# Hybrid attention and mixture-of-experts layer: the gate's low-rank columns join another product, and the blocks of the last norm take other turns

## The chip, the cores and the metric

The kernel runs on one core of one Trainium2 chip. The metric is the device time of one execution in microseconds (us); lower is better. A core has five engines that work from queues of their own and wait for one another through semaphores: TensorE (PE, matrix products; loads of its stationary operand are listed as PEld), VectorE (DVE), ScalarE (ACT), GpSimd (POOL) and SyncE (SP). SBUF is the core's working memory, PSUM the small memory that products write to, HBM the main memory. All transfers share 16 DMA engines.

## The reference

One decoder layer over 2048 tokens of 1024 numbers, in float32, and a last norm. Cut to what the change touches:

```python
n = rmsnorm(h, norm1_g)
proj = n @ w_in                       # (2048 x 1024) @ (1024 x 3088)
gq, gk, gv, gr, glr, aq, ak, av = jnp.split(proj, IN_SPLITS, axis=-1)   # gr: 512 columns, glr: 16
log_a = jax.nn.log_sigmoid(glr @ gla_gate_w2 + gla_gate_b) / GLA_TAU    # low-rank forget gate
...                                   # linear attention, its output times silu(gr); dilated window attention
h = h + o @ w_out
h = h + hier_moe(rmsnorm(h, norm2_g), ...)
return rmsnorm(h, final_norm_g)

def hier_moe(n, ...):                 # 4 groups of 8 experts: one group a token, two experts in it
    ...
    hb = silu(xb @ w1[e]) * (xb @ w3[e])     # 1024 -> 512
    return hb @ w2[e]                        # 512 -> 1024, times the gate, summed into the token
```

A token's group is the best of four, and both its experts are of that group. So a token of group 0 or 1 is finished after expert 15, one of group 2 after expert 23, one of group 3 after its later expert.

## The kernel before, in words

**Products in float32.** An operand is split into a rounded part (hi) and the rest (lo), and each product is made of three: hi with hi, hi with lo, lo with hi.

**The front (`front`).** The tokens are normed in 16 tiles of 128 (`norm_tile`) and transposed into quarters of 512 tokens, `nh` and `nl`. Columns of `w_in` come in groups of 256 (`w_group`): load into `raw`, split on ScalarE (hi) and VectorE (lo). `tmajor` makes tiles of tokens by columns: for 128 tokens 8 x 3 products of 256 columns, two such tiles in one PSUM bank, one eviction of 512 columns. `dmajor` makes columns by tokens. The PSUM ring for these products (`mps`, tiles named mm) has three banks. `gla_cols(h)` does the columns of the linear attention for one half of the tokens (two quarters): first 2 x 256 columns of gr, then `lowrank` for each quarter, then gq, gk, gv. `lowrank` multiplies the 16 columns glr (hi and lo side by side, 32 stationary columns `wg`) with the 512 tokens of a quarter: 16 products of 512 columns (L244, L245), a copy to SBUF (L249), then a small product with `w2` (L254) that is written twice, for hi and lo, and the gate's Exp and Ln (L259, L260). The work yields after a few products; `weave` puts pieces of other work (norms of the next tiles, or the chunks of the linear attention) between the yields by shares written by hand, and a scheduler then orders each engine's queue by a timeline that it simulates.

**The experts (`moe`).** 32 experts, one after the other. An expert has 160 slots for tokens: 128 in one tile, 32 more (R, `nr`) handled by narrow products (L1367, L1423). Its 6 MB of weights come in six loads of 1 MB (L1303) into six `raw` buffers, each split on ScalarE and VectorE (L1308). `up` does w1 and w3 and the gating product h (L1372, L1373), `across` transposes h (L1385, L1388), `down` does w2 (L1407 to L1409), evicts the result y on VectorE and ScalarE (L1413, L1411), and adds it into the rows of the tokens in HBM (`acc`) by two adding transfers from POOL's queue (L1415 for 128 slots, L1427 for the other 32).

**The last norm, in turns.** Once all tokens are routed, `order` sorts them by classes: tokens of groups 0 and 1, of group 2, of group 3 without the last two experts, and the rest, whose tokens are in the last two experts (`late[:, 3]`). The sorted tokens make 16 blocks of 128. A block of a class may be taken once the class's last expert has added: `TIERS` says from which expert on, and `turns` gives one block to each expert from there. `take` gathers a block from `acc` (L1249), `scale` squares and sums it on ScalarE (L1262), makes the factor on VectorE and POOL (L1263, L1264), `give` multiplies (L1270) and writes the rows to the output (L1272). A block taken at one expert is scaled behind that expert's evictions and given behind those of the next. The blocks from NB = 13 on are taken after the last expert's adds. Behind is a note to the scheduler (`behind`) that names what comes first in a queue; data dependencies hold besides.

Of the kernel before, what the change touches and what calls it, by code (L numbers as in the profile page):

```python
# [17 lines left out]
T = 2048  # L18
# [14 lines left out]
         (30, range((T - 8 * SLOTS // 2) // 128, (T - 2 * SLOTS) // 128), 30))  # L33
NB = (T - 2 * SLOTS) // 128
# [26 lines left out]
class Layer:  # L61
# [24 lines left out]
    def pool(self, st, name, bufs, **k):  # L86
        return st.enter_context(self.tc.tile_pool(name=name, bufs=bufs, reuse_waits="tile", **k))
# [48 lines left out]
    def front(self):  # L136
        tc, nc, a = self.tc, self.nc, self.a
        with ExitStack() as st:
# [33 lines left out]
            def split_w(c0, n, hi, lo):  # L172
                src = a["w_in"][0].rearrange("(k p) c -> p k c", p=128)
                for u in range(2):
                    ks = slice(4 * u, 4 * u + 4)
                    raw = wp.tile([128, 4, n], F32, name=f"raw{n}", bufs=3)
                    nc.scalar.dma_start(raw, src[:, ks, c0:c0 + n])
                    nc.scalar.copy(hi[:, ks], raw)  # L178
                    nc.vector.tensor_tensor(lo[:, ks], raw, hi[:, ks].bitcast(F32), OP.subtract)  # L179

            def w_group(c0):
                hi = wp.tile([128, KD, 256], F32R, name="whi")
                lo = wp.tile([128, KD, 256], F32R, name="wlo")
                split_w(c0, 256, hi, lo)
                return hi, lo
# [21 lines left out]
            def tmajor(w, q, dst, col0):  # L207
                hi, lo = w
# [26 lines left out]

            def lowrank(q):

                if q % 2 == 0:
                    self.wg = wp.tile([128, KD, 32], F32R, name="wg", bufs=1)
                    split_w(COL["glr"], 16, self.wg[:, :, 0:16], self.wg[:, :, 16:32])  # L240
                wg = self.wg
                ps = mps.tile([128, 512], F32, name="mm")
                for k in range(KD):
                    nc.tensor.matmul(ps[0:32], wg[:, k, :], nh[q][:, k, :], start=k == 0, stop=False)  # L244
                    nc.tensor.matmul(ps[0:32], wg[:, k, :], nl[q][:, k, :], start=False, stop=k == KD - 1)  # L245
                    if k % 2:
                        yield 0.86
                glrT = sp.tile([32, 512], F32, name="o")
                nc.scalar.copy(glrT, ps[0:32])  # L249
# [16 lines left out]
            def gla_cols(h):  # L266
                qs = (2 * h, 2 * h + 1)
                for i in range(2):
                    w = w_group(COL["gr"] + 256 * i)
                    for q in qs:  # L270
                        yield from tmajor(w, q, self.gs, 256 * i)
# [31 lines left out]
            w2 = keep.tile([32, 256], F32, name="w2")  # L303
            nc.scalar.dma_start(w2[0:16], a["gla_gate_w2"][0])
            nc.scalar.dma_start(w2[16:32], a["gla_gate_w2"][0])
# [697 lines left out]
    def route(self, rt, sps, lg, t0, B, cum, ids, iota, islot, ebase, tokid, tokm, tri, one):  # L1003
# [89 lines left out]
        V.tensor_tensor(self.late[:, 3, t0:t0 + B], Mc[:, :, NE - 2], Mc[:, :, NE - 1], OP.max)  # L1093
# [91 lines left out]
    def moe(self):  # L1185
        tc, nc, a = self.tc, self.nc, self.a
        with self.moest as st:
# [249 lines left out]
            turns = {e + n: j for _, js, e in TIERS for n, j in enumerate(js)}  # L1437
            waiting = None
            for e in range(NE):
# [3 lines left out]
                block = None  # L1443
                if e in turns:
                    block = take(turns[e], gp.tile([128, D], F32, name="x"))
                    self.behind(block[2], self.sums[1], "a block's turn is behind the expert's own work")
# [17 lines left out]
                if block:  # L1464
                    waiting = block[0], block[1], scale(block[1], (self.evicted[0], self.evicted[1], self.sums[1]))
# [3 lines left out]
            give(*waiting)  # L1469
# [115 lines left out]
```

## Time and profile before

| | |
|---|---|
| median of 3 runs | 2213.71 us (2210.59 to 2214.66) |
| the profiled execution | 2214.42 us |
| its span in the profile | 2212.6 us |
| granted TensorE clock, mean | 0.972 of 2.4 GHz |
| TensorE, VectorE, ScalarE, GpSimd busy | 2096.8, 1272.2, 1057.2, 530.6 us |
| DMA, moved over the span | 436.59 MB, 197 GB/s |

The span is what the engines' records cover; the execution's own time is 1.8 us longer. Busy time of TensorE is the time in which a product is under way; products overlap, so the distance between their starts says what one costs. In a timeline a row has the start, the duration, engine, line and operation, out<-in by the program's names and the shape; behind it, in brackets, how long the engine stood idle before and what ended that. Landing is the end of a transfer.

### The profile page before, as it was taken

Reading aid. Unit: us, or ns where it says so; the run is one execution under the profiler, and the core shown is the slowest. Engines: PE = TensorE matmul, PEld = TensorE weight load, DVE = VectorE, ACT = ScalarE, POOL = GpSimd, SP = SyncE. Lnnn points to the kernel's source line nnn. Section 1 sums busy time; section 2 is a strip of 40 time slices with the busy share of each in tenths; the row PEclk is TensorE's granted clock in tenths of the full one; section 3 lists DMA queues with packets and bytes.
Section 4 is the critical chain, followed back from the end, with each engine's and each line's share of the span. In section 5 each row is a group of like instructions: output and inputs, shape, how many; then the busy total and the mean of one; then the engine's idle time right before and its main releaser. Section 6 shows DMA issues by size and latency. Waiting matters only on the chain.

```text
span 2212.6 us, 38640 instructions
## 1 busy us (share of the span) xinstructions
PE 2096.8 (95%) x15306; PEld 1571.0 (71%) x15306; DVE 1272.2 (57%) x2469; ACT 1057.2 (48%) x1809; POOL 530.6 (24%) x370
## 2 busy tenths in 40 slices
PE   7999999999997999999999968999999999999993
PEld 7799889799885666666667756666767766666662
DVE  5203346424435556666646775676767677766762
ACT  5412335522323367767723334465555556555651
POOL 2000000000002002441421253632222344424432
PEclk9999999999998999999989969999999999999996
DMA  8333333333325614453358827788878889988973
GB/s 252 109 127 102 115 117 117 98 113 124 96 85 179 192 68 134 150 132 92 96 174 283 253 100 249 253 315 300 291 278 301 310 307 351 329 303 294 319 276 106
DMA packets 189033, 436.59 MB, mean 197 GB/s; under 512 B 35041, under 2 KB 106530, under 8 KB 162978
## 3 DMA queue, kind: packets, MB, share of 16 engines
q1 hardware_dynamic: 139090, 347.65, 44.5%
q0 software_dynamic: 21488, 60.36, 10.3%
q10 hardware_dynamic: 28272, 26.09, 4.0%
q8 instruction: 122, 2.00, 0.4%
q14 instruction: 61, 0.50, 0.1%
HBM read 342.48 MB, written 92.08 MB: 196 GB/s over the span
## 4 chain that ended last, share of the span: by engine, by line
PE 83%; DMA 6%; DVE 4%; issue 2%; POOL 2%; ACT 1%; SPq 0%; ACTq 0%; DVEq 0%; POOLq 0%
PE r L1367 5%; PE s L561 5%; PE mm L1360 5%; PE mm L1358 5%; PE mm L1359 4%; PE mm L216 4%; PE mm L217 4%; PE mm L193 4%; PE mm L218 4%; PE mm L194 4%; PE mm L195 4%; PE po L590 4%; PE pt L575 4%; PE mm L1407 3%; PE mm L1408 3%; PE r L1423 3%
## 5 line engine op out<-in xcount | busy, mean ns | idle before, releaser
L1308 DVE TENSOR_TENSOR lo<-raw,hi 128x2048 fp32r<-128x2048 f32 x192 | 438.3, 2290 | 133.0 <-ACT hi L1308 132.3
L1308 ACT CAST hi<-raw 128x2048 fp32r<-128x2048 f32 x192 | 364.6, 1905 | 191.7 <-DMA raw<-expert_w 170.8
L567 ACT ACTIVATE P<-P,st 128x256 f32<-128x256 f32 (+1 forms) x384 | 173.9, 455 | 96.9 <-DVE st L565 92.6
L216 PE MATMUL mm<-whi,nh 128*128 128x256 f32 x768 | 219.9, 286 | 0.0
L218 PE MATMUL mm<-whi,nl 128*128 128x256 f32 x768 | 218.2, 284 | 0.0
L217 PE MATMUL mm<-wlo,nh 128*128 128x256 f32 x768 | 217.8, 284 | 0.0
L1360 PE MATMUL mm<-lo,nh 128*128 128x512 f32 x512 | 206.6, 405 | 1.1 <-DVE lo L1308 1.1
L1358 PE MATMUL mm<-hi,nh 128*128 128x512 f32 x512 | 205.0, 401 | 1.7 <-ACT nh L1336 1.3
L1359 PE MATMUL mm<-hi,nl 128*128 128x512 f32 x512 | 201.6, 394 | 0.0
L131 POOL TENSOR_TENSOR ss<-ss,mhalf 128x1 f32<-128x1 f32 (+1 forms) x32 | 28.9, 902 | 695.2 <-DVE ss L130 695.1
L565 DVE CUSTOM_DVE_ANT_0 P<-s,amask 128x256 f32<-128x256 f32 (+1 forms) x384 | 124.9, 362 | 66.2 <-PE s L561 42.9
L193 PE MATMUL mm<-nh,whi 128*128 128x512 f32 x384 | 154.5, 402 | 0.0
L194 PE MATMUL mm<-nl,whi 128*128 128x512 f32 x384 | 153.1, 399 | 0.0
L195 PE MATMUL mm<-nh,wlo 128*128 128x512 f32 x384 | 152.7, 398 | 0.0
L1367 PE MATMUL r<-raw,nr 128*32 128x256 f32 x2048 | 148.5, 383 | 0.0
L216 PEld LDWEIGHTS mm<-whi,nh 128*128 128x128 f32 x768 | 145.5, 189 | 2.0 <-issue 0.7
L217 PEld LDWEIGHTS mm<-wlo,nh 128*128 128x128 f32 x768 | 145.6, 190 | 0.8 <-DVE wlo L179 0.4
L218 PEld LDWEIGHTS mm<-whi,nl 128*128 128x128 f32 x768 | 144.9, 189 | 0.1
L1415 POOL DMA_INDIRECT acc<-y,it x32 | 84.6, 2642 | 205.6 <-ACT y L1411 195.8
L561 PE MATMUL s<-k,q 64*128 64x256 f32 (+1 forms) x768 | 132.8, 416 | 0.4 <-DVE st L565 0.3
L1360 PEld LDWEIGHTS mm<-lo,nh 128*128 128x128 f32 x512 | 96.6, 189 | 42.7 <-issue 14.0
L179 DVE TENSOR_TENSOR wlo<-raw,whi 128x1024 fp32r<-128x1024 f32 x48 | 57.0, 1220 | 112.7 <-ACT whi L178 112.7
(345 smaller groups left out, 4252.3 us busy)
## 6 DMA issues: line engine op xcount, KB each, us to landing
raw<-expert_w SPq DMA_DIRECT2D x192, 1024.0 KB, 9.7
raw<-w_in ACTq DMA_DIRECT2D x48, 512.0 KB, 5.0
fb<-fac SPq DMA_DIRECT2D x24, 384.0 KB, 7.5
x<-x SPq DMA_DIRECT2D x16, 512.0 KB, 5.0
og<-og SPq DMA_DIRECT2D x32, 256.0 KB, 3.8
xr<-x SPq DMA_DIRECT2D x32, 256.0 KB, 3.2
v<-av SPq DMA_DIRECT2D x8, 1024.0 KB, 7.2
hp<-xr SPq DMA_DIRECT2D x32, 256.0 KB, 2.3
```

The source lines that it names most:

```text
L193: nc.tensor.matmul(ps, hi[:, k, ms], nh[q][:, k, :], start=k == 0, stop=False)
L194: nc.tensor.matmul(ps, hi[:, k, ms], nl[q][:, k, :], start=False, stop=False)
L195: nc.tensor.matmul(ps, lo[:, k, ms], nh[q][:, k, :], start=False, stop=k == KD - 1)
L216: nc.tensor.matmul(ps[:, j, :], h, hi[:, k, :], start=j == 0 and k == 0, stop=False, skip_group_check=True)
L217: nc.tensor.matmul(ps[:, j, :], h, lo[:, k, :], start=False, stop=False, skip_group_check=True)
L218: nc.tensor.matmul(ps[:, j, :], l, hi[:, k, :], start=False, stop=k == KD - 1, skip_group_check=True)
L561: nc.tensor.matmul(ps[:, h, 0:w], KQ[p, br][hs, 128 * blk:128 * blk + 128], keys(br, blk, KQ[p, "k"][hs]), start=True, stop=True, skip_gro ...
L1308: split = nc.scalar.copy(hi, raw), nc.vector.tensor_tensor(lo, raw, hi.bitcast(F32), OP.subtract)
L1358: nc.tensor.matmul(ps[m], nh[:, k, :], hi[:, kk, :], start=k == 0, stop=False)
L1359: nc.tensor.matmul(ps[m], nl[:, k, :], hi[:, kk, :], start=False, stop=False)
L1360: nc.tensor.matmul(ps[m], nh[:, k, :], lo[:, kk, :], start=False, stop=k == KD - 1)
L1367: nc.tensor.matmul(pr[32 * g:32 * g + 32], nr[:, k, :], raw[:, k % 4, (g % 2) * 256:(g % 2) * 256 + 256], start=k == 0, stop=k == KD - 1, ...
```

## The change

It has two parts.

The 16 columns glr no longer have products of their own. In `gla_cols` the first group of gr is loaded with them as a group of 272 columns (`w_group` with `more`), and `tmajor_more` makes tiles of 128 tokens by 272 columns, each in a PSUM bank of its own: 256 columns go through Silu as before, 16 are copied to `gl`. `lowrank` transposes four of these 128x16 pieces, and goes on as before with `w2` of 16 rows in place of 32.

The last class of the last norm is the last expert's tokens alone. NB becomes 14. The third class has three blocks, taken at expert 31, the last: two of them are scaled in front of `down` and given there, the third is given behind the adds. The eleven blocks of the first two classes are spread over experts 16 to 29 (16, 17, 18, 20, 21, 22, 24, 25, 26, 28, 29; before 16 to 21, 24 to 28, and 30 and 31 for the third class). Two blocks in place of three stay behind the last adds.

```diff
-         (30, range((T - 8 * SLOTS // 2) // 128, (T - 2 * SLOTS) // 128), 30))
-NB = (T - 2 * SLOTS) // 128
+         (31, range((T - 8 * SLOTS // 2) // 128, (T - SLOTS) // 128), 31))
+NB = (T - SLOTS) // 128
...
+            def w_group(c0, more=None):
+                hi = wp.tile([128, KD, 272], F32R, name="whi")
+                lo = wp.tile([128, KD, 272], F32R, name="wlo")
...
+                    nc.scalar.dma_start(raw[:, :, 0:256], src[:, ks, c0:c0 + 256])
+                    if more is not None:
+                        nc.scalar.dma_start(raw[:, :, 256:272], src[:, ks, more:more + 16])
...
+            def tmajor_more(w, q):
+                hi, lo = w
+                glr[q] = sp.tile([128, 4, 16], F32, name="gl", bufs=2)
+                for t2 in range(2 * q, 2 * q + 2):
+                    o = sp.tile([128, 2, 256], F32, name="o")
+                    for j in range(2):
+                        ps = mps.tile([128, 512], F32, name="mm")
+                        t = (2 * t2 + j) % 4
+                        for k in range(KD):
+                            h, l = nh[q][:, k, t * 128:t * 128 + 128], nl[q][:, k, t * 128:t * 128 + 128]
+                            nc.tensor.matmul(ps[:, 0:272], h, hi[:, k, :], start=k == 0, stop=False)
+                            nc.tensor.matmul(ps[:, 0:272], h, lo[:, k, :], start=False, stop=False)
+                            nc.tensor.matmul(ps[:, 0:272], l, hi[:, k, :], start=False, stop=k == KD - 1)
...
+                        nc.scalar.activation(o[:, j], ps[:, 0:256], AF.Silu)
+                        nc.vector.tensor_copy(glr[q][:, t, :], ps[:, 256:272])
...
             def lowrank(q):
-                for k in range(KD):
-                    nc.tensor.matmul(ps[0:32], wg[:, k, :], nh[q][:, k, :], start=k == 0, stop=False)
-                    nc.tensor.matmul(ps[0:32], wg[:, k, :], nl[q][:, k, :], start=False, stop=k == KD - 1)
+                for t in range(4):
+                    nc.tensor.transpose(ps[0:16, t * 128:(t + 1) * 128], glr[q][:, t, :], self.ident)
...
-            turns = {e + n: j for _, js, e in TIERS for n, j in enumerate(js)}
+            ends = [e for _, _, e in TIERS[1:]] + [NE]
+            turns = {}
+            for (_, js, e), end in zip(TIERS, ends):
+                for n, j in enumerate(js):
+                    turns.setdefault(e + n * (end - e) // len(js), []).append(j)
...
+                if e == NE - 1:
+                    done = [(j, x, scale(x, self.crossed)) for j, x, _ in blocks]
+                    for d in done[0:2]:
+                        give(*d, after=(self.crossed[1],))
                 down(w2, h, itA[:, e], (irA[:, e], i4A[:, e:e + 1]), e)
...
+                if e == NE - 1:
+                    give(*done[2], after=(self.evicted[1], self.sums[1]))
```

On TensorE's queue, at the low-rank gate of the first half, the rows before were these (nh and nl are the tokens, wg the weights of the 16 columns; the pair repeats eight times for a quarter):

```order
L244 MATMUL mm<-nh,wg 32x512
L245 MATMUL mm<-nl,wg 32x512
L254 MATMUL mm<-w_176,o 128x256 x4
L244 MATMUL mm<-nh,wg 32x512
L245 MATMUL mm<-nl,wg 32x512
```

After the change the same place reads (gl are the copied 16 columns, ident the unit matrix; the first two rows are the second group of gr, and the last is the first product of gq):

```order
L218 MATMUL mm<-wlo,nh 128x256
L219 MATMUL mm<-whi,nl 128x256
L266 MATMUL mm<-ident,gl 16x128 x4
L274 MATMUL mm<-w_176,o 128x256 x4
L266 MATMUL mm<-ident,gl 16x128 x4
L274 MATMUL mm<-w_176,o 128x256 x4
L194 MATMUL mm<-nh,whi 128x512
```

The 16 products of a quarter are gone, and between the two products with `w2` four transposes are left.

On POOL's queue, from the last two gathers of the experts' time to the writes at the end, the rows before were:

```order
L1249 DMA x<-acc,soon 128x1024 x2
L1415 DMA acc<-y,it 2177x1024
L1427 DMA acc<-yr,i_13065 8708x256
L1264 TENSOR_TENSOR ss<-ss,mhalf 128x1
L1415 DMA acc<-y,it 2177x1024
L1427 DMA acc<-yr,i_13065 8708x256
L1272 DMA out<-x,places 2048x1024
L1264 TENSOR_TENSOR ss<-ss,mhalf 128x1
L1249 DMA G<-acc,places 128x1024 x3
L1272 DMA out<-x,places 2048x1024
L1264 TENSOR_TENSOR ss<-ss,mhalf 128x1
L1272 DMA out<-G,places 2048x1024
```

After the change it starts with the adds of expert 30 (L1436 is the add of 128 slots, L1448 of 32, L1270 a gather, L1293 a write, L1285 the power of the factor):

```order
L1436 DMA acc<-y,it 2177x1024
L1448 DMA acc<-yr,i_13038 8708x256
L1293 DMA out<-x,places 2048x1024
L1270 DMA x<-acc,soon 128x1024
L1270 DMA G<-acc,soon 128x1024
L1270 DMA x<-acc,soon 128x1024
L1285 TENSOR_TENSOR ss<-ss,mhalf 128x1
L1293 DMA out<-x,places 2048x1024
L1285 TENSOR_TENSOR ss<-ss,mhalf 128x1 x2
L1293 DMA out<-x,places 2048x1024
L1436 DMA acc<-y,it 2177x1024
L1448 DMA acc<-yr,i_13038 8708x256
```

The gathers moved from in front of expert 30's adds to behind them, and two writes now stand in front of expert 31's. Behind the last row follow the third write, two gathers, and a power and a write for each.

On ScalarE's queue the last expert read before (L1372 and L1378 are Silu, L1388 the split of the transposed h, L1411 the eviction of y, L1262 a block's square):

```order
L1308 CAST hi<-raw 128x2048 x4
L1372 ACTIVATE h<-mm 128x512
L1378 ACTIVATE hr<-r 64x256
L1388 CAST hh<-mm 128x512
L1411 ACTIVATE y<-mm,it 128x512
L1262 ACTIVATE junk,ss<-x 128x1024
L1262 ACTIVATE junk,ss<-G 128x1024 x3
```

and reads after (L1393, L1399, L1409, L1432 and L1283 are the same five):

```order
L1393 ACTIVATE h<-mm 128x512
L1329 CAST hi<-raw 128x2048
L1399 ACTIVATE hr<-r 64x256
L1409 CAST hh<-mm 128x512
L1283 ACTIVATE junk,ss<-x 128x1024 x2
L1283 ACTIVATE junk,ss<-G 128x1024
L1432 ACTIVATE y<-mm,it 128x512
L1283 ACTIVATE junk,ss<-G 128x1024 x2
```

Three squares moved in front of the last eviction of y, and two in place of four stand behind it.

## Rows read from the trace of the kernel before

**Rows 1.** Busy time by stretch; then granted clock, DMA share, GB/s

```profile
core 0: us, PE busy (x) PEld busy (x) DVE busy (x) ACT busy (x) POOL busy (x), PEclk, DMA share, GB/s
20.00:690.00 670.00, 668.67 (x5264) 589.22 (x5264) 255.43 (x493) 237.95 (x353) 25.33 (x29) 1.00 0.36 114
1345.00:1770.40 425.40, 421.26 (x2994) 294.62 (x2996) 295.66 (x234) 236.51 (x180) 135.42 (x70) 0.99 0.83 293
1770.40:2176.90 406.50, 394.71 (x2774) 271.51 (x2769) 285.72 (x223) 225.68 (x189) 160.52 (x78) 0.99 0.84 299
2140.00:2162.00 22.00, 22.00 (x142) 15.71 (x135) 15.12 (x12) 13.13 (x11) 7.99 (x5) 1.00 0.97 361
2163.00:2176.00 13.00, 11.26 (x78) 7.44 (x76) 6.16 (x7) 2.75 (x4) 0.00 (x0) 0.87 0.01 1
```

**Rows 2.** Timeline at the low-rank gate of the first half

```profile
66.84 0.28 PE L216 MATMUL mm<-whi,nh 128*128 128x256 f32 x1
...
70.80 0.28 PE L216 MATMUL mm<-whi,nh 128*128 128x256 f32 x1
...
71.15 0.39 PE L244 MATMUL mm<-nh,wg 128*32 128x512 f32 x1
...
74.60 0.39 PE L245 MATMUL mm<-nl,wg 128*32 128x512 f32 x1
75.03 0.57 ACT L249 COPY o<-mm 32x512 f32<-32x512 f32 x1 [1.20 <-PE mm L245]
75.66 1.99 PE L254 MATMUL mm<-w,o 32*128 32x256 f32 x8 [0.67 <-ACT o L249]
...
78.27 0.63 ACT L259 ACTIVATE e<-e 128x512 f32<-128x512 f32 x1 [1.27 <-DVE e L258]
```

**Rows 3.** Evictions of y (L1411) by stretch, from expert 3 and from expert 16

```profile
1443.40:1770.50 327.10, 8.93 (x14) 1.00 0.84 297
1770.50:2148.90 378.40, 9.37 (x15) 0.99 0.87 309
```

**Rows 4.** Chain of waits at the last expert: start, us, what

```profile
2149.72 12.58 DMA raw<-expert_w
...
2166.54 0.69 DVE h L1373
...
2170.55 0.43 PE mm L1407
```

**Rows 5.** Timeline of POOL and TensorE around the last expert

```profile
2140.36 0.96 POOL L1249 DMA_INDIRECT x<-acc,soon  x1 [0.30 <-issue]
2140.71 1.04 PE L1333 MATMUL tp<-ident,G 128*128 128x128 f32 x8
...
2153.09 3.42 POOL L1427 DMA_INDIRECT acc<-yr,i  x1 [0.30 <-issue]
...
2167.28 0.66 PE L1385 MATMUL mm<-ident,h 128*128 128x128 f32 x4 [1.33 <-DVE h L1373]
```

**Rows 6.** Transfers issued from 2137, 2149 and 2185 us: median us to landing

```profile
x<-acc,soon POOLq DMA_INDIRECT x2, 11.1
...
acc<-yr,i POOLq DMA_INDIRECT x1, 9.9
...
G<-acc,places POOLq DMA_INDIRECT x3, 5.5
```

**Rows 7.** Timeline of the tail

```profile
2176.15 0.69 ACT L1411 ACTIVATE y<-mm,it 128x512 f32<-128x512 f32 x1 [7.59 <-PE mm L1409]
2176.74 1.04 ACT L1262 ACTIVATE junk<-x 128x1024 bf16<-128x1024 f32 x1
2177.13 1.59 POOL L1415 DMA_INDIRECT acc<-y,it  x1 [20.01 <-ACT y L1411]
...
2197.78 2.03 POOL L1272 DMA_INDIRECT out<-G,places  x1 [0.18 <-issue]
2200.11 0.97 POOL L1272 DMA_INDIRECT out<-G,places  x1 [0.30 <-POOLq L1475]
```

**Rows 8.** Line L1427 on POOL: duration in ns, least, median and most

```profile
L1427 POOL DMA_INDIRECT acc<-yr,i x32: 1552/2858/3588, 1357.4 to 2179.0; - x32
```

More of the change, by code (lines that the diff above doesn't have):

```diff
@@ L207, in tmajor @@
             def tmajor(w, q, dst, col0):
-                hi, lo = w
+                hi, lo = (t[:, :, 0:256] for t in w)
                 for t2 in range(2 * q, 2 * q + 2):
@@ L234, in tmajor @@
                     yield 0.65
+            glr = {}
+            def tmajor_more(w, q):
[11 more added lines that the diff above has]
+                            nc.tensor.matmul(ps[:, 0:272], l, hi[:, k, :], start=False, stop=k == KD - 1)
+                            if k % 2 and k < KD - 1:
+                                yield 0.69
+                        nc.scalar.activation(o[:, j], ps[:, 0:256], AF.Silu)
+                        nc.vector.tensor_copy(glr[q][:, t, :], ps[:, 256:272])
+                        yield 0.69
+                    o4 = o.rearrange("p j (h v) -> p (j h) v", v=128)
+                    nc.vector.tensor_tensor(o4, o4, gn.unsqueeze(1).broadcast_to((128, 4, 128)), OP.mult)
+                    nc.sync.dma_start(self.gs[t2 * 256:(t2 + 1) * 256, 0:256].rearrange("(j p) c -> p j c", p=128), o)
@@ L248, in lowrank @@
-                glrT = sp.tile([32, 512], F32, name="o")
-                nc.scalar.copy(glrT, ps[0:32])
+                for t in range(4):
+                    nc.tensor.transpose(ps[0:16, t * 128:(t + 1) * 128], glr[q][:, t, :], self.ident)
+                glrT = sp.tile([16, 512], F32, name="o")
+                nc.scalar.copy(glrT, ps[0:16])
+                yield 0.5
                 for t2 in range(2):
@@ L267, in gla_cols @@
                 qs = (2 * h, 2 * h + 1)
[L268 to L271, printed above, removed]
+                w = w_group(COL["gr"], COL["glr"])
+                for q in qs:
+                    yield from tmajor_more(w, q)
+                w = w_group(COL["gr"] + 256)
+                for q in qs:
+                    yield from tmajor(w, q, self.gs, 256)
                 for q in qs:
@@ L1092, in route @@
         V.tensor_copy(self.late[:, 0:3, t0:t0 + B].rearrange("p g b -> p b g"), goh[:, :, 1:4])
-        V.tensor_tensor(self.late[:, 3, t0:t0 + B], Mc[:, :, NE - 2], Mc[:, :, NE - 1], OP.max)
+        V.tensor_copy(self.late[:, 3, t0:t0 + B], Mc[:, :, NE - 1])
         def scatter(b, k):
@@ L1442, in moe @@
                     G[e + 2] = gather(e + 2)
[L1443 to L1446, printed above, removed]
+                blocks = []
+                for n, j in enumerate(turns.get(e, ())):
+                    blocks.append(take(j, gp.tile([128, D], F32, name="x") if n < 2 else gp.tile([128, D], F32, name="G", bufs=3)))
+                    self.behind(blocks[-1][2], self.sums[1], "a block's turn is behind the expert's own work")
                 if e % 4 == 0 and e + 2 < NE:
@@ L1463, in moe @@
                 waiting = None
-                if block:
-                    waiting = block[0], block[1], scale(block[1], (self.evicted[0], self.evicted[1], self.sums[1]))
+                if e == NE - 1:
+                    give(*done[2], after=(self.evicted[1], self.sums[1]))
+                if blocks and e < NE - 1:
+                    waiting = blocks[0][:2] + (scale(blocks[0][1], (self.evicted[0], self.evicted[1], self.sums[1])),)
                 if e == 1:
@@ L1468, in moe @@
             last = [take(j, gp.tile([128, D], F32, name="G", bufs=3)) for j in range(NB, NT)]
-            give(*waiting)
             for j, x, _ in last:
```

24 lines of the change are left out of this document (6 added, 18 removed).

## Prediction

> **What bounds the kernel now.** I read the table by stage first: from 20 to 690 us TensorE is busy in 668.7 of 670 us while DMA stands at 0.36 and VectorE and ScalarE below half, so every TensorE instruction taken out there is time [rows 1]. From 1345 us, in the experts, DMA is at 0.83 to 0.84 and TensorE still at 97 to 99% [rows 1]. Then the evictions of the second products give the pace of an expert: between the fourth and the seventeenth, where no block of the last norm has its turn, 14 evictions take 327.1 us, 25.16 us for each of the 13 steps; from the seventeenth to the 31st 378.4 us for 14 steps, 27.03 us each [rows 3]. These 14 steps, which hold 13 gathers of blocks and 11 writes, cost 26.2 us above the earlier pace: turns are not free.
>
> Then the chain of waits at the end. The last MB of w2 of expert 31 takes 12.58 us to land, until 2162.30; its two splits stand ahead of the gating product on VectorE, which starts at 2166.54, and TensorE continues at 2167.28 [rows 4]. After the idle time its products step by 0.43 us instead of 0.23: the clock there is 1.2 of 2.4 GHz (the granted clock from 2163 to 2176 is 0.87) [rows 1, 4]. Last the tail: from the last product to the end are 36 us in which TensorE does nearly nothing: the last two adds, their landing, three gathers, norms and writes, one after the other on POOL's queue [rows 7].
>
> **The change part by part.** *The gate's low-rank columns ride on a 272-column product.* Removed: 64 products of 512 columns (L244 and L245, 16 for each quarter). 16 of them start from 71.15 to 74.60, so 0.230 us each [rows 2]: 64 x 0.230 = 14.7 us. Added: 384 products are 16 columns wider. 256 columns step by 0.120 us (33 products from 66.84 to 70.80) [rows 2], so a column costs (0.230 - 0.120)/256 = 0.43 ns, and 384 x 16 of them 2.6 us. Added too: 16 transposes of a 128x16 piece, bounded by the 128x128 ones (8 in 1.04 us [rows 5], so up to 0.13, stepping by 0.11): 1.8 us; below, a step per column of the output would make it a little less. In the first half nothing lies between the two quarters' low-rank work any more, and on ScalarE the second quarter's copy stands behind the first quarter's Exp, which ended at 78.90 [rows 2]. The products of 75.66 to 77.65 plus four transposes leave TensorE ready at 78.1, and with the copy of 0.57 it goes on at about 79.5: 1.5 us of waiting where 0.67 stood before, so 0.8 more. In the second half chunks of the linear attention lie between. The four narrow loads of the 16 columns are the same ones as before, earlier. The splits' 16 extra columns, the smaller evictions (16 more Silus of half size) and 16 copies of 128x16 lie on engines less than half busy [rows 1]; if that cover were gone they would cost their own length, some 0.2 to 0.4 us each. Sum of this stage: -14.7 + 2.6 + 1.8 + 0.8 = **-9.5 us**, bounds -10.7 (no new wait) and -6 (TensorE waits for a bank in each of the 16 new ones for 0.2 us). The number of attention chunks left over when the columns run out is the same before and after, so the stretch from 690 to 1345 us stays as it is.
>
> The Trainium skill, "TensorE: Matmul & The Clock Gate", section "Back-to-back issue gap", states a sustained spacing of about 131 ns for 512 columns, by which the 64 products were worth only 8.4 us. The trace does not agree: they step by 230 ns [rows 2], and the row decides.
>
> *Turns spread, three moved behind the weights.* Before, the gathers of the last two early blocks, the second at 2140.36, take 11.1 us to land [rows 5, 6], while the weights of expert 31 come in; from 2140 to 2162 DMA is 0.97 busy at 361 GB/s [rows 1]. After, all three gathers (and, behind them on POOL, the powers, two writes and expert 31's adds) wait for the adds of expert 30, which land 9.9 us after 2153.09, at 2163.0 [rows 5, 6], when DMA is at 0.01 [rows 1]. That takes 2 x 0.52 MB out of the saturated stretch, 2.9 us at 361 GB/s; the write of the block before, which now falls to expert 30, puts 0.52 MB back, 1.45 us. So the last weights land about 1.45 us earlier. TensorE was ready at 2165.95 [rows 5], so 1.3 us of waiting goes, and with it perhaps the half clock (ten products at the lower level, about 1.6 us). Gain 1.3 to 2.9: I take **-2.1**, for bounds 0 (the loads are released by TensorE, not by DMA) and -2.9. The spread itself I cost at 0: eleven turns lie on the experts before and after; their gaps move from the 23rd, 24th and 30th expert to the 20th, 24th, 28th and 31st. The bounds come from the turns' own price, 26.2/13 = 2.0 us: two turns better or worse, -4 to +4.
>
> *The tail.* One gather, one norm and one write fewer behind the last landing. The second write of the last class stood at 2197.78 because the third block's power came first; without it it starts near 2197.0, and the last write at 2200.11 is gone [rows 7]: -3.1. Against that, ScalarE, VectorE and POOL carry three norms in front of the last evictions. With the gathers at about 2163.9, 2165.2 and 2166.5 (one behind the other, as in the tail) and landings like those of the three in the idle tail, median 5.5 [rows 6] and somewhat more for the third, the last lands near 2172.7. Two squares of 1.04 with their readouts end near 2175.2, before the eviction at 2176.15 [rows 7], so ScalarE is not late. VectorE's multiplies follow, and POOL, which must issue the second write ahead of the last two adds, gets there near 2177.1 and to the add near 2178.4 instead of 2177.13 [rows 7]: +1.3. **-1.8 us**, bounds -3.1 (the norms hide entirely) and +1 (the writes also stand in front of the adds on the DMA queue).
>
> Sum: -9.5 - 2.1 - 1.8 = -13.4, against the profiled execution's own 2214.42 (span 2212.6): **2201.0 us**. The median of the three runs is 0.7 lower, within what runs differ by.
>
> **The rivals.** *Only the columns count* (0.20): the last weights land when they did, since their issue waits for TensorE to release the buffers, and the adds' slip eats the shorter tail. For it: that chain names the load from its issue at 2149.72 on, and that waited for the buffer [rows 4]. 2214.4 - 9.5 = 2204.9. *POOL is held at the end* (0.10): an add's issue on POOL takes 1.55 at the quiet end but 2.86 us in the median of 32 [rows 8]; if the writes and adds of the last stage, issued beside VectorE's multiplies, take the long time, two of them put 2.6 us on the path: 2203.6. By the Trainium skill, "SBUF — State Buffer", section "Who interferes with whom", VectorE and GpSimd exclude each other from one shared pair of ports for whole instructions, which is this mechanism; the two durations fit it. *The spread pays* (0.14): with a free expert after each three the loads catch up, and two or three turns' price returns: 2201 - 6 = 2195. *Slower* (0.03): a bank of the products' PSUM ring now fills in 24 x 0.127 = 3.05 us instead of 6, and is free only after both the Silu and the copy; with three banks TensorE waits when an eviction ends more than 6.1 us after its product. Each of 16 banks would have to be 7.2 us late to cost 18 us and end at 2219; ScalarE is busy 238 of 670 us there [rows 1], which speaks against it. *No change* (0.03): smaller waits of that kind eat the 13 us.
>
> **How the numbers follow.** My forecast has 0.50 and covers 2197.5 to 2204. The range is 2194 to 2208.5: it takes in the paying spread and the first two rivals with half the bound of -6 for the columns. A measurement of this kernel can tell 0.2%, 4.4 us. All cases but the last two are faster: 0.92, allowing for the edges; same 0.05; slower 0.03.
>
> **What would show it.** No rows of the two low-rank products; the stages to 690 us shorter by 9 to 10 us with TensorE still without idle time. The last load of expert 31 landing some 1.5 us sooner after the eviction of expert 30, and no half clock in its second products. Three gathers right behind expert 30's adds; the last add's issue 0 to 1.5 us later after the last product; two writes behind it, the span ending 3 us sooner after the landing. Wrong would make it: idle time in front of the 272-column products, the pace of experts 16 to 30 off 27 us by more than 0.3, or the last eviction waiting for a square.

## The result, and the profile after

The changed kernel took 2200.99 us, median of 14 runs (2197.74 to 2210.34), the kernel before beside it 2214.18, median of 14 (2209.78 to 2218.52): ratio 0.9948, 95% interval 0.9936 to 0.9959. The forecast was 2201.0. It was right in the sum and wrong in the terms: in the traces the front, forecast 9.5 us shorter, is 2.3 us shorter, and the experts with turns, forecast 2.1, are 11.5.

The profiled execution has a span of 2197.6 us, 15.0 less than before, at a mean clock of 0.971. Where the 15.0 us lie is read from the starts of the same instructions in both traces, the last product of the front's columns and four evictions of y on ScalarE (us; differences in brackets):

| stage | before | after |
|---|---|---|
| to the start of the last column product | 688.4 | 686.1 (-2.3) |
| from there to the eviction of expert 16 | 1081.9 | 1081.8 (-0.1) |
| experts 17 to 28 | 320.9 | 319.2 (-1.7) |
| expert 29 | 32.3 | 25.9 (-6.4) |
| experts 30 and 31 | 52.7 | 49.3 (-3.4) |
| last eviction to the end | 36.4 | 35.4 (-1.0) |

Busy time by stretch after the change (columns as in [rows 1]; the last row goes from the eviction of expert 16 to that of expert 31):

```profile
20.00:690.00 670.00, 664.67 (x5233) 590.19 (x5233) 257.75 (x507) 238.57 (x360) 25.42 (x29) 0.98 0.36 115
75.60:85.80 10.20, 9.48 (x24) 6.13 (x23) 4.15 (x6) 7.78 (x9) 0.00 (x0) 0.50 0.49 150
399.90:406.60 6.70, 6.70 (x25) 5.31 (x24) 2.66 (x4) 2.49 (x4) 0.00 (x0) 0.50 0.52 157
410.10:413.40 3.30, 3.30 (x8) 2.63 (x9) 1.16 (x4) 3.21 (x4) 1.02 (x1) 0.50 0.43 126
1767.80:2162.20 394.40, 387.32 (x2778) 268.51 (x2782) 285.08 (x224) 227.38 (x191) 159.45 (x81) 1.00 0.87 310
```

The front was at a granted clock of 1.00 before [rows 1]. Now it has three stretches at 0.50, that is 1.2 GHz, 20.5 us together, while the experts, at 0.99 before, are at 1.00. The first of these stretches begins at the low-rank gate, here TensorE and ScalarE at the place of [rows 2]:

```profile
71.31 0.60 PE L266 MATMUL mm<-ident,gl 128*16 128x128 f32 x4
71.51 0.60 ACT L225 ACTIVATE o<-mm 128x512 f32<-128x512 f32 x1 [5.11 <-PE mm L219]
72.00 1.98 ACT L184 CAST whi<-raw 128x1024 fp32r<-128x1024 f32 x2
73.89 0.57 ACT L268 COPY o<-mm 16x512 f32<-16x512 f32 x1
74.51 2.79 PE L274 MATMUL mm<-w,o 16*128 16x256 f32 x8 [2.60 <-ACT o L268]
78.97 3.78 PE L274 MATMUL mm<-w,o 16*128 16x256 f32 x8 [0.72 <-ACT o L268]
82.67 0.80 PE L194 MATMUL mm<-nh,whi 128*128 128x512 f32 x1
83.26 0.63 PE L195 MATMUL mm<-nl,whi 128*128 128x512 f32 x1
```

ScalarE's copy, for which the w2 products wait, stands behind a Silu and two casts of the next weights. Before, 16 products of 3.7 us lay over these; now four transposes of 0.6 us do, and TensorE is idle for 2.60 us. Behind that it runs at the lower level: eight records of w2 products take 2.79 and 3.78 us where they took 1.99 [rows 2]. The second half has the same wait, 1.90 us. The lines view from 20 to 690 us adds the waits up (busy us, mean ns of one; idle us in front), 1.3 us in the kernel before:

```profile
L274 PE MATMUL mm<-w,o 16*128 16x256 f32 x32 | 12.1, 540 | 5.2 <-ACT o L268 5.2
```

At the other end, the three experts that won most, expert 29 to 31, in a window of before:

```profile
2091.10:2176.10 85.00, 80.83 (x551) 55.93 (x554) 52.85 (x42) 40.38 (x34) 25.84 (x12) 0.94 0.66 222
```

and of after:

```profile
2087.00:2162.20 75.20, 74.73 (x533) 51.53 (x536) 52.64 (x44) 42.18 (x40) 29.09 (x15) 1.00 0.75 255
```

Before, TensorE was idle for 4.2 of 85.0 us and 10.2 us were at 1.2 GHz; after, 0.5 us and none. That is most of the 9.8 us that these experts gain: 3.7 us of waiting, and some 5 us of slow products. The window after also holds 18 products fewer (533 against 551). They stand ahead of it, so a little of expert 29's gain is work that moved into the experts before. Where expert 29 lost its time before, ScalarE's timeline shows, and below it TensorE's second products:

```profile
2103.86 0.60 ACT L1372 ACTIVATE h<-mm 128x512 f32<-128x512 f32 x1 [3.88 <-PE mm L1360]
2104.35 1.90 ACT L1308 CAST hi<-raw 128x2048 fp32r<-128x2048 f32 x1
2109.75 1.90 ACT L1308 CAST hi<-raw 128x2048 fp32r<-128x2048 f32 x1 [3.50 <-DMA raw<-expert_w]
2111.68 0.38 ACT L1378 ACTIVATE hr<-r 64x256 f32<-64x256 f32 x1
2112.08 0.59 ACT L1388 CAST hh<-mm 128x512 fp32r<-128x512 f32 x1
2112.72 0.73 PE L1407 MATMUL mm<-hi,hh 128*128 128x512 f32 x2 [1.63 <-ACT hh L1388]
```

and after, at the same expert:

```profile
2096.53 0.60 ACT L1393 ACTIVATE h<-mm 128x512 f32<-128x512 f32 x1 [1.35 <-PE mm L1381]
2102.38 0.38 ACT L1399 ACTIVATE hr<-r 64x256 f32<-64x256 f32 x1 [5.25 <-PE r L1388]
2103.47 0.59 ACT L1409 CAST hh<-mm 128x512 fp32r<-128x512 f32 x1 [0.71 <-PE mm L1406]
2105.57 1.90 ACT L1329 CAST hi<-raw 128x2048 fp32r<-128x2048 f32 x1 [0.60 <-DMA raw<-expert_w]
```

Before, two casts of weights stand between the Silu of h and the hh that TensorE waits for, and the second waits 3.50 us for its load. After, the scheduler has put none there.

The tail of [rows 7], after (L1285 is the power of a block's factor, L1291 the multiply):

```profile
2162.20 0.67 ACT L1432 ACTIVATE y<-mm,it 128x512 f32<-128x512 f32 x1
2162.44 1.29 DVE L1291 SCALAR_TENSOR_TENSOR x<-x,ss,fg 128x1024 f32<-128x1024 f32 x1
2162.63 1.50 POOL L1285 TENSOR_TENSOR ss<-ss,mhalf 128x1 f32<-128x1 f32 x1 [0.60 <-DVE ss L1284]
2164.16 1.28 DVE L1291 SCALAR_TENSOR_TENSOR G<-G,ss,fg 128x1024 f32<-128x1024 f32 x1 [0.44 <-POOL ss L1285]
2164.31 2.04 POOL L1293 DMA_INDIRECT out<-x,places  x1 [0.18 <-issue]
2166.66 1.60 POOL L1436 DMA_INDIRECT acc<-y,it  x1 [0.30 <-issue]
2168.56 1.58 POOL L1448 DMA_INDIRECT acc<-yr,i  x1 [0.30 <-issue]
2174.31 0.98 POOL L1270 DMA_INDIRECT G<-acc,places  x1 [2.88 <-DMA acc<-yr,i]
2185.67 1.03 POOL L1293 DMA_INDIRECT out<-G,places  x1 [1.61 <-DVEq L1507]
```

The first of the last adds is issued 4.46 us after the last eviction starts, 0.98 before [rows 7]: it slips by 3.5 us. From the second add to the last write are 17.1 us, 21.1 before (2179.03 to 2200.11). The other 0.5 us of the tail lie behind the start of the last write.

### The profile page after: what moved, and what is told of

It is laid out like the page before. It is cut to its first block, busy times and chain, and to the rows that moved or that the text cites. A ratio compares the mean times of both kernels' runs of the same rounds, so it can differ in the third digit from the quotient of the medians.

```text
span 2197.6 us, 38549 instructions
## 1 busy us (share of the span) xinstructions
PE 2081.0 (95%) x15258; PEld 1564.8 (71%) x15258; DVE 1273.2 (58%) x2481; ACT 1057.4 (48%) x1813; POOL 529.7 (24%) x370
## 5 line engine op out<-in xcount | busy, mean ns | idle before, releaser
L217 PE MATMUL mm<-whi,nh 128*128 128x256 f32 x640 | 182.3, 285 | 0.0
L218 PE MATMUL mm<-wlo,nh 128*128 128x256 f32 x640 | 180.6, 282 | 0.0
L219 PE MATMUL mm<-whi,nl 128*128 128x256 f32 x640 | 179.5, 280 | 0.0
L1388 PE MATMUL r<-raw,nr 128*32 128x256 f32 x2048 | 147.1, 383 | 0.0
L1436 POOL DMA_INDIRECT acc<-y,it x32 | 84.7, 2647 | 155.9 <-ACT y L1432 147.0
L185 DVE TENSOR_TENSOR wlo<-raw,whi 128x1024 fp32r<-128x1024 f32 (+1 forms) x48 | 57.1, 1227 | 111.4 <-ACT whi L184 111.4
L217 PEld LDWEIGHTS mm<-whi,nh 128*128 128x128 f32 x640 | 120.0, 188 | 2.0 <-issue 0.7
L219 PEld LDWEIGHTS mm<-whi,nl 128*128 128x128 f32 x640 | 121.1, 189 | 0.1
L218 PEld LDWEIGHTS mm<-wlo,nh 128*128 128x128 f32 x640 | 120.3, 188 | 0.1
```

What stands on the lines that cost most here:

```text
L217: nc.tensor.matmul(ps[:, j, :], h, hi[:, k, :], start=j == 0 and k == 0, stop=False, skip_group_check=True)
L218: nc.tensor.matmul(ps[:, j, :], h, lo[:, k, :], start=False, stop=False, skip_group_check=True)
L219: nc.tensor.matmul(ps[:, j, :], l, hi[:, k, :], start=False, stop=k == KD - 1, skip_group_check=True)
L1388: nc.tensor.matmul(pr[32 * g:32 * g + 32], nr[:, k, :], raw[:, k % 4, (g % 2) * 256:(g % 2) * 256 + 256], start=k == 0, stop=k == KD - 1, ...
```

## The experiments

They ran in four groups, each beside the kernel before on one chip, where its median was 2223.3, 2211.5, 2213.1 and 2223.5 us. So ratios stand here, and between groups lengths of stages from the traces. The experts 1 to 3 are left out of those, for a reason told with the second.

**One part alone.** Each half of the change was put on the kernel before.

```diff
  e1: gla_cols, w_group, tmajor_more, lowrank, w2 as changed; turns as before
  e2: TIERS, NB, late, turns, the branch at NE - 1 as changed; front as before
```

> The kernel before with the 272-column products alone (no change to the last norm). Theory (the removed products had been the cover of ScalarE's casts, TensorE now waits and its granted clock falls): the work ahead of the experts is only some 2.4 us shorter, so about 2211.8 us, 2209 to 2214, with waits of about 2.6, 0.7 and 1.9 us in front of the w2 products and a granted clock of 1.2 GHz behind them. The account of the prediction: 9.5 us shorter, 2204.7. Rival (the experts gained because all of it came 2.4 us sooner, so that loads and turns met differently): most of the whole change's 13 us are here, 2202 to 2204, though the front itself is only 2.4 shorter.

Measured: ratio 0.9947 (0.9928 to 0.9965), by medians -11.0 us. In its trace the last column product starts at 683.8, 4.6 us sooner than in the trace of before, with waits of 5.2 us and 17.1 us at 1.2 GHz; expert 29 takes 31.0 us. So in the trace the front has the small gain and the experts the old stall, as the theory has it, but the time says more than twice as much.

> The kernel before with the change of the last norm alone (turns spread, last class one expert, three norms inside expert 31; front as before). Theory: the experts with turns and the tail hold nearly all of the gain, 11.5 and 1.0 us, so 2201.7 us, 2199.5 to 2204.5. The account of the prediction: 2.1 and 1.8 us, 2210.3. Rival (the experts' gain hangs on the 2.4 us by which the front comes sooner): 2206 to 2212.

Measured: ratio 0.9963 (0.9951 to 0.9974), by medians -6.7. In the trace the experts 17 to 31 take 395.5 us (405.9 before, 394.4 after), the tail 35.7: the experts' gain does not hang on the front. The time is smaller than the theory's, and the trace has one thing the edit does not touch, a hold in expert 1 (the view of waits from 1396 to 1424 us; what waited, for what, us, times, longest):

```profile
ACT hr L1378 <- remote: 11.7, 1, 11.7
```

The trace names no instruction of the core that ends it. Waits of this kind, 2 to 12 us in the experts 1 to 3, are in the traces of five experiments on the chips where the kernel before takes 2223 us, and in none of the others. The two halves (-18 us together) do not add up to the whole (-13) measured elsewhere; beside a kernel before of 2223 us all ratios seem lower by some 0.003, and as no trace of the kernel before was taken there, that stays open.

**The low-rank gate.** Two edits of the changed kernel: transposes and copy moved ahead of one quarter of the second gate group each, so that no wait is left (e3); or only ScalarE's casts put behind the copies (e4).

```diff
 e3  for q in qs:
+        yield from lowrank_turn(q)           # transposes and copy
         yield from tmajor(w, q, self.gs, 256)
     for q in qs:
         yield from lowrank(q)                # the w2 products
 e4  cast = nc.scalar.copy(hi[:, ks, 0:n], raw[:, :, 0:n])
+    self.behind(cast, self.copied, ...)      # for gq
```

> The changed kernel with the transposes of the low-rank columns and their copy on ScalarE issued earlier, each ahead of one quarter of the second gate group, so that some 5.7 us of products lie between the transposes and the w2 products. Theory: the waits of 2.6, 0.7 and 1.9 us go and with them the stretches at 1.2 GHz, so the front is 6 to 8 us shorter than in the changed kernel: 2194 us, 2192.5 to 2196. Rival (the waits count, the clock does not): 5 us or less, 2196 to 2197. Rival (what the front wins is lost in the stretch from 690 to 1345 us or in the experts): no change, 2199 to 2203.

> The changed kernel in which only ScalarE's casts of the next weights stand behind the low-rank copies. Theory: the copy of the first quarter starts about 1.9 us sooner, and TensorE's wait of 2.6 us falls to 0.7 to 0.9; if a wait of that length leaves the granted clock at 2.4 GHz the first half wins 1.9 us and some 3 to 4 us of half clock, and so about 2195 to 2198 with the second half's part; if the clock falls at a short wait too, only 2 to 3.5 us, 2197.5 to 2199. Rival (the casts, now 4 us later, hold up the gq products): no gain, 2200 to 2203.

Measured: e3 0.9879 (0.9858 to 0.9901), e4 0.9892 (0.9870 to 0.9913). The last column product starts at 676.7 and 676.5, 9.4 and 9.6 us sooner than in the changed kernel, where the expectations had 6 to 8 us (e3) and at most 6 (e4). In e4 the two waits of the first half are 0.71 and 0.66 us, and the clock falls there all the same, for 10.2 us; in the second half it does not. In e3 one step of the theory failed: there is no idle time, and the clock fell twice, each time for 6.8 us. TensorE's timeline at the first fall, first and last rows:

```profile
71.45 4.46 PE L279 MATMUL mm<-w,glT 16*128 16x256 f32 x16
75.84 0.80 PE L194 MATMUL mm<-nh,whi 128*128 128x512 f32 x1
...
81.36 0.40 PE L195 MATMUL mm<-nl,whi 128*128 128x512 f32 x1
```

and the window of the first fall (granted clock 0.50):

```profile
74.30:81.10 6.80, 6.80 (x17) 4.83 (x16) 4.63 (x7) 4.49 (x5) 0.00 (x0) 0.50 0.66 197
```

It fell in a row of w2 products, 4.46 us long, that use 16 rows of the array. At the second fall, from 395.1 us, some products of the attention's chunks (64x64) stand between the w2 products:

```profile
391.28 1.99 PE L279 MATMUL mm<-w,glT 16*128 16x256 f32 x8
393.20 0.85 PE L423 MATMUL lev<-X 64*64 64x64 f32 x14
393.98 1.13 PE L279 MATMUL mm<-w,glT 16*128 16x256 f32 x4
```

So no wait is needed for a fall; what these two share is the w2 products of two quarters close together. The next kernel therefore keeps the two quarters' w2 products apart; it ran beside the changed kernel, and once more in a later group:

```diff
 e8  for q in qs:
         yield from lowrank_turn(q)
         yield from tmajor(w, q, self.gs, 256)
+        yield from lowrank(q)
```

> The changed kernel unaltered, beside the kernels of this call on one chip. The two halves alone gave -11 and -7 us beside a kernel before of 2223 us, 9 us more than beside the changed kernel (2214). If the chips differ in the first experts, where the traces of the halves show engines held up by nothing but a remote event (2 to 12 us in the experts 1 to 3), the ratio lies between 0.991 and 0.995 and the profile again shows the front only 2 to 5 us shorter and the experts from the 16th on 9 to 12 us shorter. If the halves add up whatever the chip, it is 0.991 to 0.992 on each chip.

> The changed kernel with transposes and copies early and the w2 products of each quarter (16 rows of the array) directly behind that quarter's second gate group, so that no two quarters' lie together. In the earlier kernel with all of them together the granted clock fell to 1.2 GHz for 6.8 us twice though TensorE had no idle time. Theory (a stretch of 4 us of 16-row products lets the clock fall, one of 2 us does not): no half clock ahead of 690 us, the front 11 to 13 us shorter than in the changed kernel, and the time 9 to 13 us below it. Rival (ScalarE's Exp and Ln with their table loads now hold the Silus and TensorE waits for a bank): less than 9 us. Rival (the gain is given back in the stretch to 1345 us): 0 to 5 us.

> The kernel with the w2 products apart once more, beside the two that follow and are built on it. It stood at 0.9881 of the kernel before (0.9860 to 0.9901) on another chip; theory: the front's gain does not hang on the chip, so 0.986 to 0.990 again, no granted clock of 1.2 GHz ahead of the linear attention's end, and expert 29 at 25.5 to 26.7 us.

Measured: the changed kernel 0.9947 (0.9926 to 0.9967), 2198.19 us, the result's ratio again and not the 0.991 to 0.992 of the halves added up; with the w2 products apart 2183.45, 14.7 us less, 0.9881 (0.9860 to 0.9901), and in the later group 0.9865 (0.9839 to 0.9890). The changed kernel's second trace has the front 3.8 us shorter than before and the experts 17 to 31 at 394.3 us, as its first (394.4). In e8 the last column product starts at 670.3, 18.1 us sooner than before and 14.3 to 15.8 sooner than in the changed kernel, without a slow stretch. That is more than the theory's 11 to 13 us for the front and 9 to 13 for the time, and leaves no room for its rivals. TensorE's timeline at the first half's second quarter:

```profile
73.39 1.99 PE L279 MATMUL mm<-w,glT 16*128 16x256 f32 x8
75.31 1.16 PE L389 MATMUL t<-tri,la 128*128 128x128 f32 x8
76.22 0.48 PE L194 MATMUL mm<-nh,whi 128*128 128x512 f32 x1
```

and its window, at a granted clock of 1.00:

```profile
68.00:80.00 12.00, 12.00 (x78) 10.66 (x78) 2.80 (x7) 8.66 (x10) 0.00 (x0) 1.00 0.34 111
```

The repeat has one fall of 3.4 us from 394.0 us, behind such a row of 1.99 us, which its expectation excluded. Two later kernels with this front (e9 and e10) have none and start the last column product at 670.9. The fronts together (idle in front of the w2 products by the lines view, time at 1.2 GHz by the record of the granted clock, start of the last column product):

| kernel | idle | at 1.2 GHz | last column product |
|---|---|---|---|
| before | 1.3 | 0 | 688.4 |
| changed | 5.2 | 20.5 | 686.1 |
| changed, again | 5.2 | 17.1 | 684.6 |
| casts behind (e4) | 1.4 | 10.2 | 676.5 |
| early transposes (e3) | 0.0 | 13.7 | 676.7 |
| w2 apart, again | 0.0 | 3.4 | 672.9 |
| w2 apart (e8) | 0.0 | 0 | 670.3 |

A product of 512 columns steps by 0.43 us at the lower level and 0.23 at the upper, so a slow us loses 0.46. From e8's 670.3 that makes 670.3 + 5.2 + 0.46 x 20.5 = 684.9 for the changed kernel (686.1), 676.4 for e4 and 676.6 for e3, each within 1.2 us of what was measured; the two repeats come out within 1.3. The kernel before has 1.3 us of waits and no slow stretch; in its first half the two quarters' w2 products, of 32 rows, had 16 products between them. Whether the 32 rows alone would have kept the clock was not tried.

**The turns.** The changed kernel with the turns close together as before, and then the same with one scheduling edge: the splits of expert 30's weights behind the crossing of expert 29 (the transposed and split h).

```diff
 e5   -  turns.setdefault(e + n * (end - e) // len(js), []).append(j)
      +  turns.setdefault(min(e + n, NE - 1), []).append(j)
 e11  +  held[30] = lambda: {p: list(enumerate(self.crossed)) for p in range(6)}
```

> The changed kernel with the turns one expert after another as before (16 to 21, 24 to 28; the last three still at 31). Theory A (five turns in a row make the loads late, and the second products of expert 29 wait): the 31 to 32 us of expert 29 come back, +5 to +7 us against the changed kernel. Theory B (the gain is from the turns of 30 and 31 that are gone from there): no difference, within 2 us. The prediction priced the spread at 0, between -4 and +4.

> The kernel with the turns close together, in which the splits of expert 30's weights stand behind the crossing of expert 29's gating product on ScalarE and VectorE (one scheduling edge for that expert; nothing else). With the turns close, as in the kernel before, two casts stand between ScalarE's first Silu and its hh of expert 29, and the second waits 3.5 us for its load; with the turns spread none stands there. Theory (what the spread was worth at expert 29 is the order of the instructions, not the bytes of the turns): expert 29 takes 25.5 to 27 us in place of 31.2, no wait of 1.6 us for hh and no half clock there, and the ratio to the kernel before goes from 0.9977 to about 0.995. Rival (the loads are late because five turns in a row take their time on the DMA queues): TensorE then waits for these weights at the start of expert 30, which takes 4 to 5 us more, and the sum of the experts 29 and 30 stays at 56 to 57 us; ratio 0.997 to 0.998.

Measured: e5 0.9977 (0.9963 to 0.9991), 7.0 us above the changed kernel beside it, as theory A has it for the time; e11 0.9921 (0.9901 to 0.9940), beside a kernel before of 2223 us. If ratios are lower there by some 0.003, as above, that is some 0.995; the traces have to decide. In e5 ScalarE and TensorE of expert 29 show the picture of before again:

```profile
2102.77 1.90 ACT L1329 CAST hi<-raw 128x2048 fp32r<-128x2048 f32 x1 [3.52 <-DMA raw<-expert_w]
2104.70 0.38 ACT L1399 ACTIVATE hr<-r 64x256 f32<-64x256 f32 x1
2105.73 0.73 PE L1428 MATMUL mm<-hi,hh 128*128 128x512 f32 x2 [1.64 <-ACT hh L1409]
```

In e11 hr stands ahead of that cast and waits for TensorE alone:

```profile
2107.53 0.38 ACT L1399 ACTIVATE hr<-r 64x256 f32<-64x256 f32 x1 [3.42 <-PE r L1388]
2108.99 0.58 ACT L1409 CAST hh<-mm 128x512 fp32r<-128x512 f32 x1 [1.08 <-PE mm L1406]
2110.37 5.68 ACT L1329 CAST hi<-raw 128x2048 fp32r<-128x2048 f32 x3
```

The experts 29 to 31 in a window of e5:

```profile
2084.20:2164.90 80.70, 77.73 (x550) 53.83 (x546) 52.78 (x43) 42.66 (x39) 25.30 (x15) 0.98 0.73 241
```

and of e11:

```profile
2089.00:2166.90 77.90, 77.08 (x550) 52.99 (x554) 53.77 (x45) 42.87 (x39) 27.81 (x16) 1.00 0.77 256
```

TensorE is idle for 3.0 us in e5, and 3.4 us are at 1.2 GHz; in e11 it is 0.8 and none. With the 75.2 us after the change, the edge gave 2.8 of 5.5 us. But these windows don't hold the same work, 550 products in e5 and e11 and 533 after. From the first of the second products of expert 16 to that of expert 31 each trace has 2754 products, in 399.6 us (e5), 396.2 (e11) and 393.1 (after): the edge gave 3.4 of 6.5 us. So the order at expert 29 is half of the spread's worth, and the loads were in time for it. The other half stays open. The theory had asked for all of it (expert 29 at 25.5 to 27; it took 30.0), the rival for nothing.

Another placement, on the kernel with w2 apart: no turn at an expert that also gathers the rows of the 32 slots (R) for the next four.

```diff
 e10  +  free = [x for x in range(e, end) if x % 4]
      +  turns.setdefault(free[min(n, len(free) - 1)], []).append(j)
```

> The kernel with the w2 products apart, with the turns at 17, 18, 19, 21, 22, 23 and 25, 26, 27, 29, 30: never at the expert that also gathers the rows of the next four, and again in rows of three with one expert free between them. Theory A (what makes expert 29 late is a long row of turns whose bytes the loads do not catch up with): 0 to -3 us, expert 29 at 25 to 27 us. Theory B (any turn at 30 makes the weights of expert 31 late again, as before): +2 to +4 us, the last load of expert 31 landing later and TensorE waiting in its second products.

Measured: 0.9883 (0.9857 to 0.9910), 5.1 us above the kernel it was built on, though the two sets of runs overlap. Both theories missed: the weights of expert 31 are in time, and by the traces 3.8 us are lost in the experts 17 to 28 (324.0 us in place of 320.2) and 2.6 in 29 to 31 (expert 29 takes 23.5 in place of 25.6, expert 30 29.4 in place of 24.3), without more idle time. What differs in the same 2754 products is their order: the narrow products of the 32 slots alternate with the others 164 times in place of 130, and the 960 of them in `up` take 72.8 us by the distances between their starts in place of 67.1. That the order is the cause is not shown. A placement is worth some 5 us, and the bytes don't say which way.

**The tail.** All three norms and writes behind the adds (e6, on the changed kernel); one ahead and two behind (e9, on w2 apart).

```diff
 e6  -  for d in done[0:2]: give(*d, after=(self.crossed[1],))
     +  for d in done: give(*d, after=(self.evicted[1], self.sums[1]))   # behind down
 e9  +  give(*blocks[0][:2], scale(blocks[0][1], self.crossed), after=(self.crossed[1],))
        down(...)
     +  for j, x, _ in blocks[1:]:                 # scaled: the eviction of yr
     +      give(j, x, scale(x, (self.evicted[0], self.scaled, self.sums[1])), after=(self.scaled, self.sums[1]))
```

> The changed kernel with the norms and writes of the three blocks behind the second products and the adds of expert 31, not in front of them. Theory (POOL's two writes and a power hold the last adds 6.4 us behind the last eviction, against 2.9 before): the adds are issued 3 to 3.5 us sooner and the end comes 2.5 to 3.5 us sooner than in the changed kernel. Rival (the three writes then stand in front of the last gathers or delay the landing on the DMA queues): no difference, or up to 2 us later.

> The kernel with the w2 products apart, in which only one of the three blocks is normed and written in front of the last second products' evictions; squares, multiplies and writes of the two others stand behind the evictions and the adds. With all three behind, the square of a late block had held the last eviction 2 to 3 us, and the writes stood in front of the last gathers. Theory (the adds wait for a square on ScalarE and for a write and a power on POOL): the last add is issued 3 to 4 us sooner after the last product, and the end comes 3 to 4.5 us sooner, about 0.15 to 0.2% below the kernel with the w2 products apart. Rival (the writes left behind the last gathers are late on POOL or on the DMA queues): 0 to 2 us.

Measured: e6 0.9959 (0.9943 to 0.9975), 3.3 us above the changed kernel, outside both expectations (2.5 to 3.5 us sooner; at most 2 later). From the last eviction to the end are 34.7 us, only 0.8 less than beside it: the second add comes 2.2 us sooner after the eviction, but three writes stand in front of the last gathers, which take 5.9 us to the first square in place of 4.5. And a square of a late block holds the eviction itself, whose products end near 2169.0:

```profile
2171.41 1.06 ACT L1283 ACTIVATE junk<-G 128x1024 bf16<-128x1024 f32 x1 [2.17 <-issue]
...
2172.47 0.67 ACT L1432 ACTIVATE y<-mm,it 128x512 f32<-128x512 f32 x1
```

In its trace 8 us are also lost between the front and expert 16, where the edit has no hand; 6.8 us more are at 1.2 GHz there. e9: 0.9855 (0.9828 to 0.9882), 2180.79 us, 3.5 us below the kernel it was built on, 2184.28, though the two sets of runs overlap (up to 2185.89, from 2182.06). Its tail is 33.0 us in place of 35.6, and the adds stand right behind the eviction at 2146.02:

```profile
2146.98 1.62 POOL L1441 DMA_INDIRECT acc<-y,it  x1 [0.78 <-ACT y L1437]
2148.91 1.58 POOL L1453 DMA_INDIRECT acc<-yr,i  x1 [0.30 <-issue]
2155.41 1.03 POOL L1275 DMA_INDIRECT G<-acc,places  x1 [3.80 <-DMA acc<-yr,i]
```

It is the fastest of all, 1.45% below the kernel before.

## Why the prediction was right, and where it was wrong

**The columns, -9.5: wrong, -2.3 and -3.8 in two traces.** The step that failed is "ScalarE's copy": the sum took it to start when the transposes end in the first quarter, and 0.8 us of new waiting in all, at the second quarter. That wait is 0.72 us in place of the 1.5 forecast; the 2.60 and 1.90 us stand in front of the first quarter's products and in the second half, where none was forecast. The 64 products were not only work but cover for a Silu, two casts of weights and the copy on ScalarE. Without them TensorE waits 5.2 us where it waited 1.3, and the clock falls for 17 to 21 us, some 8 to 9 us lost, which no term had. The waits are not the whole reason of the falls: with no wait left and the two quarters' w2 products still close together (e3) 13.7 us stay slow, and with these apart (e8) none. So the 64 products had also kept the rows of w2 products apart. The working had seen that nothing lies between the two quarters any more, and set no price on it. The expectation "TensorE still without idle time" was the sign named for it. With cover and clock restored the part gives -18.1 and -15.4, more than the forecast's own bound of -10.7, because the waits of 1.3 us go too and the 2.6 us set for the wider products don't show: the 2304 products of 256 columns, of which 384 have 272 in e8, take 285.8 us before and 285.5 in e8, by the distances between their starts. Some 3 us of the gain are in other products and not assigned.

**The spread, 0 with bounds of 4: wrong, and outside them.** Close turns cost 7.0 us by time and 5.5 at the experts 29 to 31. The working gave a turn one price, 2.0 us, wherever it stands; half of what it missed is that turns are planned instructions, and another table gives another order on ScalarE, with or without a cast that waits for its load ahead of hh; the other half is open. The pace of the experts 17 to 30, named as a sign of being wrong if it left 27 us by more than 0.3, went from 27.03 to 26.4 us.

**The last weights, -2.1: about right.** With the spread taken out (e5), the experts 30 and 31 take 49.5 us against 52.7 before and 51.5 in e1: -2.0 to -3.2. The last weight load of expert 31 lands in 8.8 us after the change, where the one on the chain took 12.58 [rows 4], and the slow stretch at 2168.9 is gone.

**The tail, -1.8: -1.0.** The shorter chain is worth 4.0, not 3.1, and the adds slip by 3.5, not 1.3: POOL's power and second write, 1.50 and 2.04 us beside VectorE's multiplies, both stand in front, and the eviction itself comes 1.1 us late behind the third square, against the step "ScalarE is not late". Elsewhere in the tail the power takes 0.57 us and the write 1.03. For the power, 1.50 us beside the multiply, this agrees with the Trainium skill, "SBUF — State Buffer", section "Who interferes with whom", by which a VectorE instruction with two inputs in SBUF contends with a GpSimd instruction that reads SBUF. What makes the write longer no run here separates.

**The rivals.** "The spread pays" came true in the experts and "POOL is held at the end" in the tail, each with a part of its price; the columns gave less than in any case but the two of 0.03. That the sum came out was luck: the columns gave 7.2 us less than their term, the experts 9.4 us more.

## What to carry to other kernels

Before a stretch of products is taken out, list what the other engines do under it, whose cover is lost with it, and what then lies close together on TensorE: here two rows of small products did, and the clock fell even where no wait was left. Where a scheduler orders the queues, a table of turns is judged by the order that it makes, at the wait that it changes, and not by the number of its turns alone. A right total proves no term; the starts of the same instructions in both traces show what each gave.

## What was not expected of the hardware

The granted clock fell to 1.2 GHz in stretches without any idle time, twice in one trace (e3): once in 4.46 us of products that use 16 of the array's rows, once where 64x64 products stood among them. The same products in rows of 1.99 us, apart, left it at 2.4 GHz in three traces (e8, e9, e10), and in a fourth one such row was followed by a fall of 3.4 us. And ScalarE was held for 11.7 us by nothing that the trace shows on its core, at the start of the experts; such holds stood in the traces of two chips and not in those of the others.
